# Opening loads in smaller parts, one of them on a second queue, and later weight splits queued differently in two attention mixers

## The chip, the cores and the metric

The kernel runs on one core of a Trainium2 chip. The metric is the device time of one execution, in microseconds (us). Before the change it is 977.02 us, the median of three runs (976.95 to 977.04).

## What is computed

A two-layer decoder trunk on 256 tokens of width 1024, all in float32. Layer 0 is a gated feed-forward half step, an attention mixer A (16 heads, a mixture of three dilated windows, which the kernel folds into one additive mask) and a second feed-forward half step. Layer 1 is the same with mixer B, whose keys and values come from one shared projection of layer 0's output. A last RMS norm follows.

```
def swiglu(h, w_gate, w_up, w_down):
    return (jax.nn.silu(h @ w_gate) * (h @ w_up)) @ w_down
...
for layer in range(DEPTH):
    h = h + 0.5 * swiglu(rmsnorm(h, ffn1_norm[layer]), ffn1_w_gate[layer], ffn1_w_up[layer], ffn1_w_down[layer])
    hn = rmsnorm(h, mix_norm[layer])
    h = h + mixer(hn)        # A or B: softmax attention, then @ w_o
    h = h + 0.5 * swiglu(rmsnorm(h, ffn2_norm[layer]), ffn2_w_gate[layer], ffn2_w_up[layer], ffn2_w_down[layer])
    if layer == 0:
        shared = shared_kv(h, kv_norm, kv_w, pos)
return rmsnorm(h, final_norm)
```

The hidden width of a feed-forward step is 2816, so its gate and up weights are 1024 x 2816 each.

## The kernel before

**Numbers in two parts.** Every product keeps float32 accuracy by splitting each operand into a coarse part and the rest. ScalarE makes the coarse part with a copy (`wh` of weights, `hi` of activations), VectorE subtracts it from the source (`wl`, `lo`), and TensorE adds up three products: coarse by coarse, coarse by rest, rest by coarse. So every weight passes through ScalarE and VectorE before TensorE may use it. `unit` (lines 152 to 169) loads 1 MB of weights with one DMA on SyncE's queue and splits it in two halves of 128 x 1024; `parts_of` (91 to 99) does the same for activations, and can put off VectorE's half.

**The stream of tokens.** `hT` holds the stream transposed, as eight blocks of 128 channels by 256 tokens. `Norm.scale` (236) multiplies a block by its gain and splits it into x; `Norm.square` (239) adds up the squares on the side; the norm's factor per token comes late and is applied to the products.

**The opening.** The first feed-forward step starts with nothing in memory. Its first two output columns of gate and up (f = 0 and 1) are therefore computed block by block, as the blocks of channels arrive: `ffn_blocks` (line 422 on) takes from `opening` (171 to 185), for each block k, the 128 x 256 parts of gate and up, and does four products of 512 columns (the coarse weights with both parts of x, line 204) and four of 256 columns (the rest of the weights, line 210) into four accumulators. The list OPENING (line 39) says how the blocks are put together: each pair (k, n) is a start and a number of blocks that share their DMAs, one buffer and one split. `first` (838 to 842) loads the x of those blocks on SyncE's queue and calls `scale` for each. The first block's weights are loaded ahead of everything on ScalarE's own DMA queue (110 to 112); they get a buffer named early. Buffers for raw weights come from a pool of four. While the first loads run, TensorE does nine matmuls on constants (117). After the blocks come the squares (line 433, ScalarE) and their additions (line 246, VectorE here), the first ordinary units for f = 2, and in the middle of its products the column sums of the norm (251).

A DMA on SyncE's queue signals one of eight semaphores in turn, and an issue waits until the DMA that last used its semaphore has landed.

**The mixers.** `mixer` (748) runs the projections and then `out_t` (613), the products of the attention's output o with w_o. The steps of the attention are put among these products by an agenda: `plan` lists for every group of four heads, at which time after its q and k are turned, which of the steps scores (s), turns (t) and values (v) of a pair of heads p is traced. `turn` (701) turns the weights of the attention, p, and splits them (706 and 709); `values` (713) computes po, which ScalarE (727) and VectorE (732) join to o; `close` splits o into the block oT (98 and 95), which `out_t` reads. The last three blocks are held back and taken together for each output.

**Order.** The order in which each engine gets its instructions is chosen when the program is built, by a scheduler that works with estimated costs; within an engine it is fixed. What the author adds to it is `queued` (144): instructions traced in its block come behind those kept under a name in `marks`, on the same engine, in order of issue only. `marks[p]` holds both halves of the split of p, `marks[("o", p)]` only VectorE's half of the split of o. The feed-forward step after a mixer names, for each half of its first units, what it is to stand behind: `queue` (lines 864 and 887) has the two halves of the first gate unit, the two of the first up unit, then those of the next units. LAST_O (line 38) is the last block o, pair 7.

Of the kernel before, what the change touches and what calls it, by code (L numbers as in the profile page):

```python
# [10 lines left out]
F32 = mybir.dt.float32  # L11
F32R = mybir.dt.float32r
AF = mybir.ActivationFunctionType
ALU = mybir.AluOpType

P = 128
S = 256
# [18 lines left out]
         ("ffn1_norm", 1), ("mix_norm", 1), ("ffn2_norm", 1)]  # L36

LAST_O = ("o", H // 2 - 1)
OPENING = ((0, 1), (1, 1), (2, 2), (4, 2), (6, 2))
GX = len(GAINS) * KD  # L40


# [25 lines left out]
def trunk(ctx: ExitStack, tc: tile.TileContext, a: dict, out: bass.AP):  # L68
    nc = tc.nc
    PS = bass.MemoryType.PSUM  # L70
    const = ctx.enter_context(tc.tile_pool(name="const", bufs=1))
    rawp = ctx.enter_context(tc.tile_pool(name="rawp", bufs=4))
# [18 lines left out]
    def parts_of(hi, lo, src, scale=1.0, later=None):  # L91

        def rest():
            if isinstance(scale, float):
                return nc.vector.tensor_sub(lo, src, hi.bitcast(F32))
            return nc.vector.scalar_tensor_tensor(lo, src, scale, hi.bitcast(F32), op0=ALU.mult, op1=ALU.subtract)  # L96

        nc.scalar.activation(hi, src, AF.Copy, scale=scale)  # L98
        (later or (lambda call: call()))(rest)

    def etile(name, dt=F32):
# [5 lines left out]

    both = const.tile([P, GX + KD * S], F32, name="gains_hT")
    gT, hT = both[:, :GX], both[:, GX:].rearrange("p (k s) -> p k s", s=S)
    early = rawp.tile([P, 2, OPENING[0][1], S], F32, tag="raw", name="raw_0_0")  # L110
    for i, n in enumerate(("gate", "up")):
        nc.scalar.dma_start(early[:, i], a[f"ffn1_w_{n}"][0][:OPENING[0][1] * P, :S].rearrange("(k p) n -> p k n", p=P))
    BF16 = mybir.dt.bfloat16
    fill = nc.const_aps.tensor(1.0, [P, 512], BF16)
    busy = trt("busy")
# [26 lines left out]
    marks = {}  # L142
# [28 lines left out]
    def opening(wg, wu, before):  # L171


        for k, n in OPENING:
            raw = rawp.tile([P, 2, n, S], F32, tag="raw", name=f"raw_0_{k}") if k else early
            wh, wl = [wp.tile([P, 2, n, S], F32R, tag=tag, name=f"{tag}_0_{k}") for tag in ("wh", "wl")]
            before(k, n)
            for i, w in enumerate((wg, wu)):
                if k:
                    nc.sync.dma_start(raw[:, i], rows(w, k, n, 0, S))  # L180
            for part in ([slice(0, 2)] if k else [slice(0, 1), slice(1, 2)]):
                marks["opening"] = [nc.scalar.activation(wh[:, part], raw[:, part], AF.Copy)]
            nc.vector.tensor_sub(wl, raw, wh.bitcast(F32))
            for j in range(n):
                yield [(wh[:, i, j, :], wl[:, i, j, :]) for i in range(2)]
# [276 lines left out]
    def ffn(name, layer, which, norm, after, first=None, beside=(), homes=("kx4", "kx6", "qkh", "qkh"), queue=()):  # L462
        wg, wu, wd = (a[f"ffn{which}_w_{n}"][layer] for n in ("gate", "up", "down"))
        sums = left_sums(homes)
        blocks = ffn_blocks(name, wg, wu, norm, first, beside, sums, queue)
        if which == 1:
            table(AF.Exp, blocks[-1][:, 0, 0:1].bitcast(F32))
        down(f"{name}_d", wd, blocks, sums, after)
# [193 lines left out]
    def attention(agenda, operands, mask, name, blocks):  # L662

        segs = [slice(t * P, t * P + (t + 1) * P) for t in range(NT)]
        owns = [slice(i * DH, (i + 1) * DH) for i in range(2)]
        sms, pTs = {}, {}

        def scores(p):
            g, b = divmod(p, HG // 2)
            (hi, lo), _ = operands(g)
            ps = [trt(f"s_{name}{p}_{i}") for i in range(2)]
            for t, seg in enumerate(segs):
                for n, (q, k) in enumerate(((hi, hi), (hi, lo), (lo, hi))):
                    for i, own in enumerate(owns):
                        nc.tensor.matmul(ps[i][:, seg], q[own, b, t, :],
                                         k[own, 2 + b].rearrange("p t n -> p (t n)")[:, :(t + 1) * P],
                                         start=n == 0, stop=n == 2)  # L680
            nm = sp.tile([P, 2, NT], F32, tag="nm", name=f"nm_{name}{p}")
            ls = sp.tile([P, 2, NT], F32, tag="ls", name=f"ls_{name}{p}")
            for i in range(2):
                sm = sms[p, i] = atile([P, 3 * P], name=f"sm_{name}{p}_{i}")
                for t, seg in enumerate(segs):
                    nc.vector.tensor_tensor_reduce(sm[:, seg], ps[i][:, seg], mask[:, seg], scale=-SCALE, scalar=3e38,
                                                   op0=ALU.add, op1=ALU.min, accum_out=nm[:, i, t:t + 1])
                agenda.after(0.7 + 0.7 * i, soften, sm, nm[:, i], ls[:, i])

        def soften(sm, nm, ls):  # L690
            for t, seg in enumerate(segs):
                nc.scalar.activation(sm[:, seg], sm[:, seg], AF.Exp, bias=nm[:, t:t + 1], scale=-1.0,
                                     accum_out=ls[:, t:t + 1])
            agenda.after(1.3, scale, sm, ls)

        def scale(sm, ls):
            nc.vector.reciprocal(ls, ls)  # L697
            for t, seg in enumerate(segs):
                nc.gpsimd.tensor_scalar(sm[:, seg], sm[:, seg], ls[:, t:t + 1], None, op0=ALU.mult)  # L699

        def turn(p, i):
            tr = trt(f"pt_{name}{p}_{i}")[:, :3 * P]
            for n in range(3):
                nc.tensor.transpose(tr[:, n * P:(n + 1) * P], sms[p, i][:, n * P:(n + 1) * P], ident)
            pT = pTs[p, i] = pp.tile([P, 2, 3 * P], F32R, tag="pT", name=f"pT_{name}{p}_{i}")
            hi = nc.scalar.activation(pT[:, 0], tr, AF.Copy)

            def rest():
                marks[p] = [hi, nc.vector.tensor_sub(pT[:, 1], tr, pT[:, 0].bitcast(F32))]

            agenda.soon(rest)

        def values(p):
            g, b = divmod(p, HG // 2)
            po = acc(f"po_{name}{p}")
            s = etile(f"o_{name}{p}")
            vs = operands(g)[1]
            acs = [po[:, i * S:(i + 1) * S] for i in range(2)]
            for i, ac in enumerate(acs):
                pT = pTs[p, i]  # L720
                v0, v1 = [flat(v[:, 2 * b + i]) for v in vs]
                for n in range(2):
                    nc.tensor.matmul(ac, v0, pT[:, n, :S], start=n == 0, stop=False)
                for n in range(2):
                    nc.tensor.matmul(ac[:, P:], v1, pT[:, n, S:], start=False, stop=n == 1)
            for own, ac in zip(owns, acs):
                nc.scalar.activation(s[own], ac[DH:], AF.Copy)
            agenda.soon(lambda: close(p, s, acs))

        def close(p, s, acs):  # L730
            for own, ac in zip(owns, acs):
                nc.vector.tensor_add(s[own], ac[:DH], s[own])
            x = atile([P, 2, S], F32R, name=f"oT_{name}{p}")

            def split():
                parts_of(x[:, 0], x[:, 1], s, later=lambda low: agenda.soon(lambda: marks.update({("o", p): [low()]})))

            agenda.soon(split)
            agenda.after(1.5, arrived, x)

        def arrived(x):
            blocks.append(x)
            if len(blocks) == KD:
                table(AF.Silu, x[:, 0, 0:1].bitcast(F32))

        return scores, turn, values
# [89 lines left out]


    def first(k, n):
        cols = slice(GX + k * S if k else 0, GX + (k + n) * S)
        nc.sync.dma_start(both[:, cols], a["gains_xT"][:, cols])  # L840
        for i in range(k, k + n):
            n0.scale(i)

    n0, n1, n2 = Norm(0, "n0", nc.vector), Norm(1, "n1"), Norm(2, "n2")
    n3, n5, n6 = Norm(4, "n3"), Norm(5, "n5"), Norm(6, "n6")
# [4 lines left out]
    w, n = a["a_w_qkv"][0], HG * DH  # L850
# [3 lines left out]
    def steps(g, *at):  # L854
        return [(wait, step, 2 * g + i) for wait, step, i in zip(at, "sstvtv", (0, 1, 0, 0, 1, 1))]

    def ending(at, apart=2.6):
        return [(at + apart * i + wait, step, 4 + i) for i in range(4) for wait, step in ((0.0, "t"), (2.3, "v"))]

    mixer("a", [qk[0], v[0], qk[1], qk[2], qk[3], v[1]],  # L860
          [steps(0, 3.0, 8.0, 11.0, 13.8, 16.5, 19.3), steps(1, 3.0, 8.0, 11.0, 13.8, 16.5, 19.3), steps(2, 4.0, 9.2),
           steps(3, 2.4, 5.4) + ending(8.4)],
          a["a_w_o"][0], masks[:, 0, :], n2, {3: 4, 4: 5})
    ffn("f20", 0, 2, n2, n3, queue=(5, 6, 7, 7) + (LAST_O,) * 4)
    kx = []
    ffn("f11", 1, 1, n3, n5, homes=("qkh", "qkh", "pT"), beside=[lambda k=k: kx.append(gain(k, 3, "kx", "kx")) for k in range(KD)])
    xkv, xq = by_token(kx), n5.xs()
# [88 lines left out]
```

## Time and profile before

| | us |
|---|---|
| median of three runs | 977.02 |
| the profiled execution | 979.19 |
| its span, first to last instruction | 977.4 |
| TensorE (PE) busy | 967.4 |
| weight loads of TensorE (PEld) busy | 833.1 |
| VectorE (DVE) busy | 813.2 |
| ScalarE (ACT) busy | 611.9 |
| GpSimd (POOL) busy | 281.4 |

The mean granted clock of TensorE over the span is 0.996 of full speed, and 174 MB are read from memory at a mean of 179 GB/s. Busy times overlap; only work that nothing else hides adds to the span. A line number such as L182 is a line of the kernel before. In the order of time, a row has its start, its length, the engine, the line, the operation, the tile written and those read, the shape, the count and in brackets how long the engine stood idle before it and what ended that; matmuls start before the one ahead of them has ended, so the distance between starts counts, not the length. Rows of a load have the issue; their last number in the list of DMAs is the time from issue to landing.

### The profile page before, as it was taken

How to read it: one execution, taken by the hardware profiler on the slowest of the kernel's cores; microseconds unless marked ns; L12 is line 12 of the kernel's file. 1: busy time of each engine (PE TensorE's matmuls, PEld its weight loads, DVE VectorE, ACT ScalarE, POOL GpSimd, SP SyncE). 2: the span in 40 equal slices, each digit the busy share in tenths (PEclk: the TensorE clock that was granted, in tenths of full speed). 3: DMA queues.
4: the chain of work that ended last, by engine and by line, in shares of the span. 5: the costliest groups of instructions: out<-in, count | busy, mean ns of one | idle time of the engine just before them, and what ended most of it. 6: DMA issues, size and time to landing. Idle time of an engine off the chain costs nothing.

```text
span 977.4 us, 14864 instructions
## 1 busy us (share of the span) xinstructions
PE 967.4 (99%) x5392; PEld 833.1 (85%) x5392; DVE 813.2 (83%) x1393; ACT 611.9 (63%) x1132; POOL 281.4 (29%) x235
## 2 busy tenths in 40 slices
PE   8999999999999999999999999999999999999997
PEld 6888888878889888888888888888888998888886
DVE  6988889887878788889898888987787778888996
ACT  7655657566777665556576655655577766666561
POOL 0211237133432211146032111622143322112451
PEclk9999999999999999999999999999999999999999
DMA  9875546664334666545855556483734345565341
GB/s 313 256 241 180 191 152 216 216 216 152 122 111 141 190 191 185 185 154 210 258 165 180 173 175 212 164 277 119 254 122 141 107 154 172 184 203 174 130 172 43
DMA packets 127145, 176.00 MB, mean 180 GB/s; under 512 B 3424, under 2 KB 106848, under 8 KB 127072
## 3 DMA queue, kind: packets, MB, share of 16 engines
q1 hardware_dynamic: 126496, 174.27, 54.9%
q8 instruction: 42, 0.69, 0.3%
q10 hardware_dynamic: 576, 0.79, 0.2%
q14 instruction: 31, 0.25, 0.1%
HBM read 173.99 MB, written 1.05 MB: 179 GB/s over the span
## 4 chain that ended last, share of the span: by engine, by line
PE 96%; DVE 1%; ACT 1%; DMA 1%; issue 0%; POOL 0%; POOLq 0%; DVEq 0%; ACTq 0%
PE f_g L204 17%; PE f_u L204 16%; PE f_u L210 9%; PE f_g L210 9%; PE dn_f_d L193 6%; PE dn_f_d L197 6%; PE dn_f_d L195 6%; PE dn_f_d_m L193 1%; PE dn_f_d_m L197 1%; PE dn_f_d_m L195 1%; PE qk_a L193 1%; PE qk_a L197 1%; PE qk_a L195 1%; PE v_a L193 1%; PE q_b L193 1%; PE ot_bo L624 1%
## 5 line engine op out<-in xcount | busy, mean ns | idle before, releaser
L386 POOL TENSOR_TENSOR j_f_u<-j_f_u,r_n 128x256 f32<-128x256 f32 x88 | 91.6, 1043 | 360.0 <-DVE j_f_u L342 339.5
L204 PE MATMUL f_g<-x_n,wh_f_g 128*128 128x512 f32 x688 | 180.6, 394 | 0.0
L204 PE MATMUL f_u<-x_n,wh_f_u 128*128 128x512 f32 x688 | 177.3, 390 | 0.0
L204 PEld LDWEIGHTS f_u<-x_n,wh_f_u 128*128 128x128 f32 x688 | 129.1, 188 | 27.2
L204 PEld LDWEIGHTS f_g<-x_n,wh_f_g 128*128 128x128 f32 x688 | 124.0, 189 | 22.8 <-DVE x_n L96 0.2
L166 DVE TENSOR_TENSOR wl_f_u<-raw_f_u,wh_f_u 128x1024 fp32r<-128x1024 f32 x86 | 113.5, 1323 | 0.8 <-ACT wh_f_u L165 0.8
L166 DVE TENSOR_TENSOR wl_f_g<-raw_f_g,wh_f_g 128x1024 fp32r<-128x1024 f32 x86 | 104.5, 1232 | 0.9 <-ACT wh_f_g L165 0.9
L210 PE MATMUL f_u<-x_n,wl_f_u 128*128 128x256 f32 x688 | 103.5, 283 | 0.0
L210 PE MATMUL f_g<-x_n,wl_f_g 128*128 128x256 f32 x688 | 102.9, 282 | 0.0
L210 PEld LDWEIGHTS f_g<-x_n,wl_f_g 128*128 128x128 f32 x688 | 96.4, 190 | 6.3
L165 ACT ACTIVATE wh_f_u<-raw_f_u 128x1024 fp32r<-128x1024 f32 x86 | 87.7, 1047 | 10.8 <-PE f_g L204 7.5
L384 ACT ACTIVATE j_f_g<-j_f_g 128x256 f32<-128x256 f32 x88 | 36.6, 417 | 89.1 <-DVE j_f_g L383 88.8
L165 ACT ACTIVATE wh_f_g<-raw_f_g 128x1024 fp32r<-128x1024 f32 x86 | 89.4, 1048 | 4.1 <-PE f_g L204 2.9
L210 PEld LDWEIGHTS f_u<-x_n,wl_f_u 128*128 128x128 f32 x688 | 91.8, 192 | 0.0
L246 POOL TENSOR_TENSOR ss_n<-ss_n,sq_n 128x256 f32<-128x256 f32 x35 | 32.5, 928 | 138.7 <-ACT sq_n L245 136.9
L98 ACT ACTIVATE act_f<-j_f_g 128x256 fp32r<-128x256 f32 x58 | 23.9, 418 | 56.5 <-DVE j_f_g L394 56.4
L394 DVE TENSOR_TENSOR j_f_g<-j_f_g,j_f_u 128x256 f32<-128x256 f32 x58 | 27.9, 486 | 29.9 <-POOL j_f_u L386 29.9
L342 DVE TENSOR_TENSOR j_f_g<-f_g,j_f_g 128x256 f32<-128x256 f32 x88 | 36.6, 416 | 11.9 <-ACT j_f_g L341 11.9
L699 POOL TENSOR_SCALAR sm_a<-sm_a,ls_a 128x128 f32<-128x128 f32 (+1 forms) x32 | 30.3, 964 | 47.8 <-DVE ls_a L697 42.1
L699 POOL TENSOR_SCALAR sm_b<-sm_b,ls_b 128x128 f32<-128x128 f32 (+1 forms) x32 | 29.1, 929 | 50.0 <-DVE ls_b L697 46.0
L341 ACT ACTIVATE j_f_u<-f_u 128x256 f32<-128x256 f32 x88 | 33.0, 375 | 14.6 <-PE row_n L263 13.6
L383 DVE TENSOR_TENSOR j_f_g<-j_f_g,r_n 128x256 f32<-128x256 f32 x88 | 41.4, 474 | 0.7
(565 smaller groups left out, 2387.3 us busy)
## 6 DMA issues: line engine op xcount, KB each, us to landing
raw_f_d<-in_ffn_w_down_dram SPq DMA_DIRECT2D x44, 1024.0 KB, 4.9
raw_f_g<-in_ffn_w_gate_dram SPq DMA_DIRECT2D x43, 1024.0 KB, 5.4
raw_f_u<-in_ffn_w_up_dram SPq DMA_DIRECT2D x43, 1024.0 KB, 5.4
raw_qka<-in_a_w_qkv_dram SPq DMA_DIRECT2D x16, 512.0 KB, 4.6
raw_va<-in_a_w_qkv_dram SPq DMA_DIRECT2D x4, 1024.0 KB, 6.1
raw_ao<-in_a_w_o_dram SPq DMA_DIRECT2D x4, 1024.0 KB, 4.9
raw_kvb<-in_kv_w_dram SPq DMA_DIRECT2D x8, 512.0 KB, 4.1
raw_qb<-in_b_w_q_dram SPq DMA_DIRECT2D x4, 1024.0 KB, 5.5
```

Source lines behind the costliest of these rows:

```text
L165: nc.scalar.activation(wh, r, AF.Copy)
L166: nc.vector.tensor_sub(wl, r, wh.bitcast(F32))
L193: nc.tensor.matmul(ac, xh, wh, start=first, stop=False)
L195: nc.tensor.matmul(ac, xh, wl, start=False, stop=False)
L197: nc.tensor.matmul(ac, xl, wh, start=False, stop=last)
L204: nc.tensor.matmul(ac, wh, flat(x), start=first and i == 0, stop=False)
L210: nc.tensor.matmul(ac[:, :S], wl, x[:, 0, :], start=False, stop=last and i == len(ws) - 1)
L342: nc.vector.tensor_add(s, ac[:, :S], s)
L383: nc.vector.tensor_mul(g, g, norm.row)
L384: nc.scalar.activation(g, g, AF.Silu)
L386: nc.gpsimd.tensor_tensor(u, u, norm.row, op=ALU.mult)
L699: nc.gpsimd.tensor_scalar(sm[:, seg], sm[:, seg], ls[:, t:t + 1], None, op0=ALU.mult)
```

## The change

Three parts.

*Opening.* Blocks 2 and 3 are no longer one entry of OPENING but two, each with its own weight DMAs, its own part of a buffer and its own split (128 x 512 instead of 128 x 1024). The first four blocks share one raw buffer, singles. The x of blocks 2 and 3 is loaded with one DMA as before, but on ScalarE's queue behind the first block's weights, and `first` leaves it out. In the built program, SyncE's queue has for these blocks gate 2, up 2, gate 3, up 3 where it had x, gate and up of both; ScalarE's queue has three DMAs ahead of its first work where it had two; the loads of the first ordinary unit and of its up half wait for other buffers. On TensorE, block 2's matmuls of coarse weights and rest alternate.

*Marks.* The function that `parts_of` hands to `later` returns both instructions, and the mark of an o keeps both: splits queued behind the last o stand behind ScalarE's copy too.

*Queue and plan.* After mixer A the second half of the first gate unit stands behind p 7, where it stood behind p 6. The values of pair 1 in mixer A are planned at 19.8 where they were at 19.3.

In the built program this gives, on ScalarE in mixer A: copy of o (pair 6), then the copies of the first gate unit's second half and of the up unit's two, then the joining of the last o and its copy, then the next unit's copy, then the loading of a function table. Before, the gate unit's second half stood right behind the last but one p, and the next unit's copy behind the table. VectorE's rests follow the same order. In mixer B, the next unit's first copy moves from ahead of the joining of the last o to behind the copy of it. The products po of pair 1 in mixer A come three matmuls of the projection later. GpSimd's order is unchanged.

```
-OPENING = ((0, 1), (1, 1), (2, 2), (4, 2), (6, 2))
+OPENING = ((0, 1), (1, 1), (2, 1), (3, 1), (4, 2), (6, 2))
...
         def rest():
             if isinstance(scale, float):
-                return nc.vector.tensor_sub(lo, src, hi.bitcast(F32))
-            return nc.vector.scalar_tensor_tensor(lo, src, scale, hi.bitcast(F32), op0=ALU.mult, op1=ALU.subtract)
+                return first, nc.vector.tensor_sub(lo, src, hi.bitcast(F32))
+            return first, nc.vector.scalar_tensor_tensor(lo, src, scale, hi.bitcast(F32), op0=ALU.mult, op1=ALU.subtract)
 
-        nc.scalar.activation(hi, src, AF.Copy, scale=scale)
+        first = nc.scalar.activation(hi, src, AF.Copy, scale=scale)
         (later or (lambda call: call()))(rest)
...
-    early = rawp.tile([P, 2, OPENING[0][1], S], F32, tag="raw", name="raw_0_0")
+
+    def load_x(engine, k, end):
+        cols = slice(GX + k * S if k else 0, GX + end * S)
+        engine.dma_start(both[:, cols], a["gains_xT"][:, cols])
+
+    singles = rawp.tile([P, 4, 2, S], F32, tag="raw", name="raw_0")
     for i, n in enumerate(("gate", "up")):
-        nc.scalar.dma_start(early[:, i], a[f"ffn1_w_{n}"][0][:OPENING[0][1] * P, :S].rearrange("(k p) n -> p k n", p=P))
+        nc.scalar.dma_start(singles[:, 0, i], a[f"ffn1_w_{n}"][0][:P, :S])
+    load_x(nc.scalar, 2, 4)
...
         for k, n in OPENING:
-            raw = rawp.tile([P, 2, n, S], F32, tag="raw", name=f"raw_0_{k}") if k else early
+            raw = rawp.tile([P, 2, n, S], F32, tag="raw", name=f"raw_0_{k}") if n > 1 else singles[:, k:k + 1].rearrange("p k i n -> p i k n")
...
             def split():
-                parts_of(x[:, 0], x[:, 1], s, later=lambda low: agenda.soon(lambda: marks.update({("o", p): [low()]})))
+                parts_of(x[:, 0], x[:, 1], s, later=lambda low: agenda.soon(lambda: marks.update({("o", p): low()})))
...
     def first(k, n):
-        cols = slice(GX + k * S if k else 0, GX + (k + n) * S)
-        nc.sync.dma_start(both[:, cols], a["gains_xT"][:, cols])
+        if k not in (2, 3):
+            load_x(nc.sync, k, k + n)
         for i in range(k, k + n):
             n0.scale(i)
...
     mixer("a", [qk[0], v[0], qk[1], qk[2], qk[3], v[1]],
-          [steps(0, 3.0, 8.0, 11.0, 13.8, 16.5, 19.3), steps(1, 3.0, 8.0, 11.0, 13.8, 16.5, 19.3), steps(2, 4.0, 9.2),
+          [steps(0, 3.0, 8.0, 11.0, 13.8, 16.5, 19.8), steps(1, 3.0, 8.0, 11.0, 13.8, 16.5, 19.3), steps(2, 4.0, 9.2),
...
-    ffn("f20", 0, 2, n2, n3, queue=(5, 6, 7, 7) + (LAST_O,) * 4)
+    ffn("f20", 0, 2, n2, n3, queue=(5, 7, 7, 7) + (LAST_O,) * 4)
```

## The prediction, on record before the changed kernel was run

> **What bounds the kernel now.** I read the page's first part, then the chain of waits at the opening, then busy time and granted clock by stage.
>
> ```profile
> span 977.4 us, 14864 instructions
> PE 967.4 (99%) x5392; PEld 833.1 (85%) x5392; DVE 813.2 (83%) x1393; ACT 611.9 (63%) x1132; POOL 281.4 (29%) x235
> ```
>
> TensorE is busy in 99% of the span, so a gain must come from its few waits. The profiled execution took 979.19 us, 1.79 more than its span and 2.17 more than the median of 977.02; I take the differences found in the span off the median.
>
> ```profile
> 0.72 3.02 DMA raw<-in_ffn_w_gate_dram
> 3.75 5.43 DMA raw<-in_ffn_w_up_dram
> 9.20 1.06 ACT wh L182
> ...
> 11.14 0.43 PE f_g L204
> ...
> 20.56 1.83 PE f_g L204 x8
> ...
> 22.73 0.70 PE f_g L210 x5
> ...
> 30.70 0.95 PE f_g L210 x8
> ```
>
> The chain (start, us, what) starts with loads: the up half of blocks 2 and 3 is issued at 3.75, lands at 9.18, is split by ScalarE, and only then TensorE goes on without a break. At 20.56 the opening's eight blocks are done. A matmul of 512 columns takes 1.83/8 = 0.23 us there, one of 256 columns 0.95/8 = 0.12; a block has four of each, 1.40 us. But at 11.14 a matmul of 512 took 0.43.
>
> ```profile
> 4.19:7.60 3.41, 2.93 (x14) 1.93 (x13) 2.56 (x6) 2.53 (x6) 0.00 (x0) 1.00 0.92 310
> 7.60:11.02 3.42, 1.59 (x9) 1.09 (x8) 1.15 (x3) 1.82 (x3) 0.00 (x0) 0.96 1.04 351
> 11.02:14.43 3.41, 3.41 (x14) 2.88 (x13) 3.25 (x6) 2.73 (x5) 0.00 (x0) 0.54 1.10 357
> ```
>
> Columns: stretch, length, busy PE, PEld, DVE, ACT, POOL, granted clock, DMA share, GB/s. PE is busy for 2.93 of 3.41 us (86%) before 7.60, then for 1.59 of 3.42 (46%), and in the stretch after that the clock is about half. So the late block costs twice: its gap, and some 1.7 us of half speed.
>
> **The opening, part by part.** Blocks 2 and 3 come one by one; their x goes on ScalarE's queue.
>
> ```profile
> GB/s 0 0 86 309 357 202 290 369 335 317 296 344 367 381 380 370 354 347 348 350 350 347 350 347 350 345 350 347 351 347 345 336 371 343 348 176 143 366 382 380
> 3.05 0.43 SPq L180 DMA_DIRECT2D raw<-in_ffn_w_gate_dram  x1
> raw<-in_ffn_w_gate_dram SPq DMA_DIRECT2D x1, 256.0 KB, 4.2
> ...
> 3.56 0.51 ACT L98 ACTIVATE x_n<-gains_hT 128x256 fp32r<-128x256 f32 x1 [0.42 <-DMA gains_hT<-in_gains_xT_dram]
> ```
>
> Rates are in steps of 0.75 us: about 350 GB/s but for a dip to 202 and 290 between 3.75 and 5.25. Bytes and their order decide. Block 2's last part now stands 1.31 MB into the order (x 156+128, the first two blocks' weights 512, x of 2 and 3 256, block 2's 256 KB) instead of 1.56. The gate half of blocks 2 and 3 stood there before and landed at 3.05 + 4.2 = 7.25. From the other side, 256 KB at 350 GB/s off 9.18 gives 8.45. I take 7.3, the row with the same bytes ahead; block 3 follows between 8.2 and 9.2. Cost: SP issues one DMA more (four weight parts for two, one x fewer) at 0.43 us, well ahead of need. ScalarE issues one more before its first work; it idles 0.42 there until block 0's x lands, and that covers it; uncovered it would be 0.43 on every block's start. The first unit's gate half no longer waits for a buffer and its up half waits only for block 3's rest; both stand behind the blocks in the queue, so this is worth nothing here. GpSimd's queue is untouched.
>
> The Trainium skill's page "Trainium Kernel Development and Optimization" (Key Constraints) speaks against the second queue: all queues run on the same 16 DMA engines, so a second issuer only saves issue time. By that rule the last landing would not move and the opening would give 0.2 us less; the trace half agrees, with a DMA share of 0.92 in the stretch to 7.60.
>
> ```profile
> 5.87 0.63 ACT L182 ACTIVATE wh<-raw 128x512 fp32r<-128x512 f32 x1 [0.69 <-DMA raw<-in_ffn_w_up_dram]
> 6.53 0.69 DVE L183 TENSOR_TENSOR wl<-raw,wh 128x512 fp32r<-128x512 f32 x1 [0.63 <-ACT wh L182]
> 10.31 0.49 PE L204 MATMUL f_g<-x_n,wh 128*128 128x512 f32 x1 [1.83 <-ACT wh L182]
> 11.38 1.06 ACT L182 ACTIVATE wh<-raw 128x1024 fp32r<-128x1024 f32 x1 [0.32 <-DMA raw<-in_ffn_w_up_dram]
> 13.59 1.06 ACT L182 ACTIVATE wh<-raw 128x1024 fp32r<-128x1024 f32 x1 [0.36 <-DMA raw<-in_ffn_w_up_dram]
> 14.68 1.23 DVE L183 TENSOR_TENSOR wl<-raw,wh 128x1024 fp32r<-128x1024 f32 x1 [0.20 <-ACT wh L182]
> 15.82 3.07 DVE L246 TENSOR_TENSOR ss_n<-ss_n,sq_n 128x256 f32<-128x256 f32 x6
> 20.28 1.22 DVE L166 TENSOR_TENSOR wl_f_g<-raw_f_g,wh_f_g 128x1024 fp32r<-128x1024 f32 x1
> ```
>
> Walk forward. Block 2: split 0.63 from 7.35, rest 0.69, ready at 8.7; block 1 ends near 8.5 (10.31 less the 1.83 of waiting). PE loses 0.2 there and block 2 runs to 10.0. Block 3, landing at 8.7, is ready at 10.0 and runs to 11.4 (11.7 if it lands at 9.2). The 1.83 us gap goes, and PE is busy from 7.60 to 11.02. Late next: blocks 4 and 5, landing at 11.3 as before (same bytes ahead): split to 12.4, rest to 13.6. Block 4 waits 1.0 us, and after three matmuls 0.5 more, to run with block 5 to 15.7. Blocks 6 and 7 bound the end: I take their landing as 13.4 instead of 13.5, since a third of the dip is filled; + 1.06 + 1.23 = 15.7, after which 1.17 of block 6 and 1.40 of block 7 remain: 18.3 instead of 20.56. VectorE then sets the pace: its additions start at 15.6 (0.2 earlier), and the six, the next unit's rest, the seventh and the second rest end at 21.3 instead of 21.5. PE needs that for the fifth L210, in the chain at 22.73 + 4 x 0.14 = 23.3; from the opening's end to that point are 2.17 + 0.56 us of its own work, so it gets there at 21.0 and waits to 21.3. **Gain 2.0 us**, 0.3 below what the opening's end alone gives.
>
> ```profile
> 22.77 0.16 DVE L253 TENSOR_SCALAR v_n<-col_n 128x2 f32<-128x2 f32 x1 [1.27 <-PE col_n L251]
> 35.65 1.22 DVE L166 TENSOR_TENSOR wl_f_u<-raw_f_u,wh_f_u 128x1024 fp32r<-128x1024 f32 x1
> 37.22 0.96 PE f_u L210 x8
> ```
>
> Does it last? VectorE's wait of 1.27 goes too, so it comes 1.5 us earlier. The tightest rest later ended at 36.87, needed by the fifth of eight at 37.7; now 35.4 against 35.7. It holds by 0.3; beyond, PE alone sets the pace.
>
> **The mixers.** Returning both instructions adds none. The marks of the last o now hold ScalarE's copy too, and the second half of mixer A's first unit waits behind the last p. The first half stays behind p 5, so its stall of p 6 stays. In the changed order the second half's copy and rest stand among the two of the up unit, ahead of the last o.
>
> ```profile
> 294.63 2.00 ACT L165 ACTIVATE wh_f_u<-raw_f_u 128x1024 fp32r<-128x1024 f32 x2
> 295.72 2.36 DVE L166 TENSOR_TENSOR wl_f_u<-raw_f_u,wh_f_u 128x1024 fp32r<-128x1024 f32 x2 [0.21 <-ACT wh_f_u L165]
> 298.00 0.84 DVE L732 TENSOR_TENSOR o_a<-po_a,o_a 64x256 f32<-64x256 f32 x2
> 298.87 0.42 ACT L98 ACTIVATE oT_a<-o_a 128x256 fp32r<-128x256 f32 x1 [1.18 <-DVE o_a L732]
> 299.32 0.42 DVE L95 TENSOR_TENSOR oT_a<-o_a,oT_a 128x256 fp32r<-128x256 f32 x1 [0.48 <-ACT oT_a L98]
> 300.37 0.28 PE L624 MATMUL ot_ao<-oT_a,wh_ao 128*128 128x256 f32 x1
> ```
>
> VectorE has three rests instead of two from 295.72, at 1.14 each (2.36 less 1.22): o_a starts at 299.14 instead of 298.00, the copy ends at 300.4, its rest at 300.9. PE needs the copy at 300.37 and the rest 0.12 later: **0.4 us lost**. Bounds: 0, if PE comes there later; 1.14, if none of the slack were there. What the move frees, ScalarE and VectorE around 290 to 293, held nobody. The v of p 1 moves behind three more matmuls, 0.7 us:
>
> ```profile
> 235.50 0.78 ACT L727 ACTIVATE o_a<-po_a 64x256 f32<-64x256 f32 x2 [1.67 <-PE po_a L725]
> ```
>
> Between 0 and 0.7 us; ScalarE idles 1.67 ahead of it, and its o is read only by the o products that follow all projections. I take nothing.
>
> ```profile
> 778.50 1.06 ACT L165 ACTIVATE wh_f_g<-raw_f_g 128x1024 fp32r<-128x1024 f32 x1 [0.52 <-PE ot_bo L625]
> 779.58 0.77 ACT L727 ACTIVATE o_b<-po_b 64x256 f32<-64x256 f32 x2
> 779.13 0.34 PE L725 MATMUL po_b<-pT_b,vs_b 128*128 128x128 f32 x2
> 781.74 0.38 PE L624 MATMUL ot_bo<-oT_b,wh_bo 128*128 128x256 f32 x1 [0.19 <-ACT oT_b L98]
> ```
>
> In mixer B a copy of 1.06 leaves the place ahead of o_b. The last po ended at 779.47, 0.1 before o_b, so o_b comes 0.1 us earlier, and with it the last oT_b, for which PE waited at 781.74: **0.1 gained** (at least nothing, at most the 0.2 of that wait). The copies pushed behind the last o delay the first x of the next stage by up to 1.1 us, hidden by the 60 o products of 0.12 us still to run, 7 us.
>
> **Sum:** -2.0 + 0.4 - 0.1 = -1.7, so 975.3.
>
> **Rivals.** The last up half of the opening took 6.8 us from issue to landing:
>
> ```profile
> raw<-in_ffn_w_up_dram SPq DMA_DIRECT2D x1, 256.0 KB, 6.8
> ```
>
> 1. *The clock falls one stretch later.* From 11.02 to 14.43 PE would now be busy for 0.4 + 0.7 + 0.8 us and some 0.5 of tails, 56% to 70%; 46% lost the clock, 86% kept it. If it falls, the stretch to 17.84 runs at half: 1.7 us back, **977.0**. The Trainium skill's page "TensorE: Matmul & The Clock Gate" (What's actually happening) has the clock halve after at least one idle window of some 3.4 us. By that rule this rival had no chance; the trace disagrees, since the clock fell after a wait of 1.83.
> 2. *The mixers cost nothing or gain*, since PE comes to the last o later than I think: **974.9**.
> 3. *Too few bytes in flight* (slower). An issue on SP waits until the DMA eight back has landed. With halves, eight hold less. If all parts took 6.8 us like that one, the last would be issued when block 2's up half lands (3.75 + 6.8 = 10.55) and land at 17.4; PE would end the opening at 22.3, 1.7 late: **979.0**. It decides from a last landing after 15.4. Against it: early parts took 4.2.
> 4. *Block 2's landing does not move* from 9.2, gap and clock stay: **977.3**, the mixers' loss alone. Against it: 256 KB less are ahead.
>
> **How the numbers follow.** Forecast 0.50 (974.8 to 975.9 by itself), rival 1 0.18, rival 2 0.22, rival 3 0.04, rival 4 0.06. The range leaves out the far part of rival 2 below and rivals 3 and 4 above: 974.5 to 977.1. A difference under 0.2% (1.95 us) is about what a measurement cannot tell from none. Faster by more needs 975.07: most of rival 2 and a quarter of the forecast, 0.34. Slower by more than 978.97: rival 3 and mishaps, 0.05. Same 0.61.
>
> **What would show it.** Right: no PE gap near 8.5 to 10.3, granted clock 1.00 from 11.02 to 17.8, end of the opening near 18.3, and in mixer A a PE wait of 0.4 for the last oT_a. Wrong: a clock of 0.5 from 14.43; a landing of blocks 6 and 7 far from 13.4; a rest of the next units that PE awaits between 20 and 40 us; no wait, or over 0.6, at the last o.

## The result, and the profile after

| | us, median | lowest to highest | executions |
|---|---|---|---|
| before, same series | 977.03 | 976.80 to 977.66 | 22 |
| after | 978.67 | 977.67 to 980.38 | 22 |

The ratio is 1.0016, 95% interval 1.0010 to 1.0023: slower by 1.6 us, where 1.7 less were forecast. The time lies 1.6 above the upper end of the range.

The page of after, first part (TensorE's busy time is again 99% of the span):

```profile
span 976.7 us, 14869 instructions
PE 966.9 (99%) x5392; PEld 831.9 (85%) x5392; DVE 812.7 (83%) x1394; ACT 611.2 (63%) x1133; POOL 282.0 (29%) x235
```

This span is 0.7 shorter than the one of before that the prediction read (977.4), and the profiled execution took 978.46, close to its median. So one profile against the other says faster, and the medians say slower. The execution of before with the profile took 979.19 against a median of 977.03; it is the odd one.

Busy time by stretch in after (PE, PEld, DVE, ACT, POOL, granted clock, DMA share, GB/s):

```profile
7.60:11.02 3.42, 3.42 (x20) 2.78 (x19) 3.00 (x7) 2.13 (x5) 0.00 (x0) 1.00 0.85 241
11.02:14.43 3.41, 2.47 (x13) 1.63 (x12) 1.92 (x3) 2.18 (x4) 0.00 (x0) 1.00 1.01 310
14.43:17.84 3.41, 3.34 (x19) 2.65 (x19) 2.51 (x5) 3.40 (x10) 0.00 (x0) 1.00 1.09 365
```

The gap between 8.5 and 10.3 is gone and the clock stays at 1.00, as predicted; block 2's copy starts at 7.39 (7.35 was worked out). But the DMA engines moved 241 GB/s from 7.60 to 11.02, where before they moved 351, and TensorE waits in the next stretch instead. The chain of waits tells why:

```profile
1.64 4.52 DMA gains_hT<-in_gains_xT_dram
6.18 0.38 SPq L186
...
8.10 5.99 DMA raw<-in_ffn_w_up_dram
14.11 1.07 ACT wh L188
15.20 1.24 DVE wl L189
...
19.34 1.86 PE f_g L210 x8
```

The x of blocks 2 and 3, on ScalarE's queue since 1.64, lands at 6.16. Only then does SyncE issue the gate half of blocks 4 and 5, at 6.18. In the profile of before it went out at 4.68:

```profile
4.68 0.43 SPq L180 DMA_DIRECT2D raw<-in_ffn_w_gate_dram  x1
```

Its semaphore is the one of that x. By the times of the releases, the eight semaphores are taken in turn over both queues, not over SyncE's alone: the issue at 3.75 in before came when block 0's gate half landed, which is on ScalarE's queue (0.72 + 3.02). All issues behind it are late too. Block 1 is later as well: ScalarE's copy of it starts at 6.45 instead of 5.87, and TensorE is busy for 2.15 us from 4.19 to 7.60 instead of 2.93. The last up half lands at 14.1 (13.4 was predicted, 13.45 in the profile of before), and the opening ends at 19.34 (18.3 predicted).

The last o of mixer A in after, VectorE's rows and then TensorE's:

```profile
294.74 1.23 DVE L172 TENSOR_TENSOR wl_f_g<-raw_f_g,wh_f_g 128x1024 fp32r<-128x1024 f32 x1 [0.21 <-ACT wh_f_g L171]
295.88 2.35 DVE L172 TENSOR_TENSOR wl_f_u<-raw_f_u,wh_f_u 128x1024 fp32r<-128x1024 f32 x2
298.15 0.84 DVE L738 TENSOR_TENSOR o_a<-po_a,o_a 64x256 f32<-64x256 f32 x2
299.47 0.43 DVE L95 TENSOR_TENSOR oT_a<-o_a,oT_a 128x256 fp32r<-128x256 f32 x1 [0.48 <-ACT oT_a L98]
```

```profile
299.26 0.28 PE L632 MATMUL ot_ao<-oT_a,wl_ao 128*128 128x256 f32 x1
299.49 0.39 PE L630 MATMUL ot_ao<-oT_a,wh_ao 128*128 128x256 f32 x1
299.95 0.39 PE L631 MATMUL ot_ao<-oT_a,wh_ao 128*128 128x256 f32 x1
```

Three rests now stand ahead of o_a, and TensorE's steps, 0.12 elsewhere in these products, are 0.23 and 0.46 here: 0.45 of waiting, for the copy and then for the rest of the last oT. In mixer B the wait of 0.19 for oT_b is gone (no bracket now):

```profile
781.12 0.38 PE L630 MATMUL ot_bo<-oT_b,wh_bo 128*128 128x256 f32 x1
```

### The profile page after: what moved, and what is told of

Read it like the earlier page. It is cut to its first block, busy times and chain, and to the rows that moved or that the text cites. A ratio compares the mean times of both kernels' runs of the same rounds, so it can differ in the third digit from the quotient of the medians.

```text
span 976.7 us, 14869 instructions
## 1 busy us (share of the span) xinstructions
PE 966.9 (99%) x5392; PEld 831.9 (85%) x5392; DVE 812.7 (83%) x1394; ACT 611.2 (63%) x1133; POOL 282.0 (29%) x235
## 4 chain that ended last, share of the span: by engine, by line
PE 95%; DVE 2%; DMA 1%; ACT 1%; issue 1%; SPq 0%; POOL 0%; ACTq 0%; POOLq 0%; DVEq 0%
PE f_g L210 16%; PE f_u L210 16%; PE f_g L216 8%; PE f_u L216 8%; PE dn_f_d L203 6%; PE dn_f_d L199 6%; PE dn_f_d L201 6%; PE dn_f_d_m L203 1%; PE dn_f_d_m L199 1%; PE dn_f_d_m L201 1%; PE qk_a L199 1%; PE qk_a L203 1%; PE qk_a L201 1%; PE v_a L199 1%; PE q_b L199 1%; PE ot_bo L630 1%
```

## The experiments

Three series on one chip each; before was run in all of them (977.21, 977.15 and 977.23). The 95% intervals of single ratios are about 0.09% (0.9 us) to each side, so for parts of half a microsecond the traces carry the argument and the medians support it: the intervals of e1, e2 and e4 all include no change. "Matmul against matmul" below means the distance in time between the starts of the same matmul in two traces.

### The kernel before, profiled again (b0_before)

No edit was made.

> The kernel before, unchanged, to see more of its executions. Theory A (the execution whose profile was read had lost the clock in the opening, and the timed executions do not): its profile here shows a granted clock of 1.00 in the stretch from 11.02 to 14.43, the opening's eight blocks done near 18.8 instead of 20.56, a span near 975.3, and the time stays 977.0. Theory B (the timed executions lose the clock too, and the change loses its time somewhere else): the clock is again near 0.54 there, the opening ends at 20.5, the span is 977.4 and the time near 979.

Measured: 977.45 (eleven executions; nine from 976.86 to 977.54, two at 978.96 and 979.13), span 975.7. Stretches, and rows of the chain:

```profile
7.60:11.02 3.42, 2.04 (x10) 1.16 (x8) 1.61 (x3) 2.03 (x4) 0.00 (x0) 1.00 1.02 357
11.02:14.43 3.41, 3.36 (x20) 2.99 (x21) 3.10 (x6) 3.08 (x6) 0.00 (x0) 1.00 1.10 358
```

```profile
8.70 1.06 ACT wh L182
9.79 1.23 DVE wl L183
...
18.80 1.85 PE f_g L204 x8
```

Theory A holds. Blocks 2 and 3 landed at 8.7 here, 0.5 earlier than in the first profile; TensorE was busy for 60% of the stretch, kept its clock, and ended the opening at 18.80 instead of 20.56. From there on the two executions run with the same distance, 1.75 us: the later landing and the half clock together. Matmul against matmul of this trace, after is 0.75 late at 60 us, 1.3 behind mixer A, and 1.15 at the end.

### Block 2 still later (e5_late_block2, e8_later_block2)

```
# first(k, n), e5: at k == 2 load the x of blocks 2 to 5, none at 4
-        cols = slice(GX + k * S if k else 0, GX + (k + n) * S)
-        nc.sync.dma_start(both[:, cols], a["gains_xT"][:, cols])
+        if k != 4:
+            cols = slice(GX + k * S if k else 0, GX + (k + n + (2 if k == 2 else 0)) * S)
+            nc.sync.dma_start(both[:, cols], a["gains_xT"][:, cols])
# e8: at k == 2 load the x of blocks 2 to 7, none at 4 and 6
```

> The kernel before, with the x of blocks 4 and 5 loaded together with that of blocks 2 and 3, so 256 KB more stand ahead of block 2's weights and none more ahead of block 4's. Block 2 should land 0.7 later than 8.68, near 9.4, and TensorE be busy for some 1.4 of 3.42 us (41%) in the stretch from 7.60 to 11.02. If a stretch under about half busy costs the clock in the next one (46% lost it, 60% and 67% kept it), the granted clock is 0.5 from 11.02 to 14.43, the opening ends near 20.7 and the time is 979.0 or more. If the clock of 0.54 in the first profile had another cause, the clock stays 1.00, the opening ends near 19.1 and the time is under 977.6.

> The kernel before with the x of blocks 4 to 7 loaded with that of blocks 2 and 3, so 512 KB more than before stand ahead of block 2's weights; nothing more ahead of the last blocks'. With 256 KB more the executions fell into two groups, 977.7 to 978.1 (six) and 979.6 to 980.6 (five), and the profiled one, in the first group, had kept its clock. If the second group are executions that lost the clock in the stretch from 11.02 to 14.43 because TensorE idled too long before it, nearly all executions are now in it, at 979.5 to 981, and the profile shows a granted clock near 0.5 in that stretch. If the groups have another cause, the profile keeps 1.00 there, and the time is under 978.5.

Measured: e5 978.14, but in two groups, six executions from 977.71 to 978.14 and five from 979.57 to 980.55. The profiled one is of the first group. e8: 980.46 (978.43 to 982.26). First e5's stretch, then e8's:

```profile
7.60:11.02 3.42, 2.09 (x10) 1.40 (x10) 2.69 (x5) 3.04 (x6) 0.00 (x0) 1.00 1.08 367
```

```profile
7.60:11.02 3.42, 1.46 (x8) 1.01 (x8) 2.35 (x5) 3.36 (x7) 0.00 (x0) 1.00 1.10 363
11.02:14.43 3.41, 3.41 (x13) 2.62 (x12) 3.41 (x5) 3.23 (x7) 0.00 (x0) 0.55 1.10 347
```

In e8 TensorE was busy for 43% of the stretch, and the next ran at 0.55: the trace ends 1.88 later than that of b0. The mean clock of every execution is on record too, and one stretch of 3.41 us at half lowers a mean over 977 us by 0.0017. In e5 the first group has 0.998 or 0.999 and the second 0.996 or 0.997. In e8 five of eight have 0.995 or 0.996; the other three kept 0.998 or 0.999 and still took 978.43, 979.01 and 980.96. So "nearly all" was not met, and e8 lost time in another way as well, which was not followed up. e5's expectation of all executions at 979.0 or more failed: it sits on the edge, the copy of block 2 starting at 8.94 in the profiled execution, not at 9.4. That copy did not wait for its weights: ScalarE first had the x of four blocks to scale, from 7.32 on.

So the kernel before has the same two kinds of execution, with the longer one rare: 6 of 126 executions in all series took over 978.9, and these six have a mean clock of 0.996 or 0.997 where the others of their series have 0.998 or more. The first profile, with 0.996, had caught one.

### The opening alone (e1_opening), on SyncE's queue (e3_opening_sp), and the second queue alone (e9_x_act)

```
# e1: the change's opening; returns of parts_of, marks, plan and queue of before
# e3: e1, but
-    load_x(nc.scalar, 2, 4)
...
-        if k not in (2, 3):
-            load_x(nc.sync, k, k + n)
+        if k != 3:
+            load_x(nc.sync, k, 4 if k == 2 else k + n)
# e9: before, but
+    nc.scalar.dma_start(both[:, GX + 2 * S:GX + 4 * S], a["gains_xT"][:, GX + 2 * S:GX + 4 * S])
...
+        if k != 2:
+            nc.sync.dma_start(both[:, cols], a["gains_xT"][:, cols])
```

> The opening's part of the change alone (blocks 2 and 3 in weight parts of their own, their x on ScalarE's queue); marks, queue and plan of the mixers as before. Theory A: slower than before, 977.5 to 978.3, since its opening ends at 19.3 against 18.8. Theory B: faster by about 1, 976.0, as the opening's end moved from 20.56 to 19.34 between the two profiles.

> The opening's part alone, but with the x of blocks 2 and 3 on SP's queue ahead of block 2's weights. If the second queue is what delays block 1's up half (5.82 before, 6.45 after), block 1 lands at 5.8 again and the time is 0.5 under that of the opening alone. If the count of DMAs in flight is what delays the last blocks (the issue that waits for the DMA eight back, a dip to 174 GB/s near 8 to 10), the last up half still lands near 14.1 and the time is that of the opening alone within 0.3.

> The kernel before with only the x of blocks 2 and 3 moved to ScalarE's queue; weights in the parts of before. If the second queue alone costs the 0.7 between the two split openings (978.03 with it, 977.34 with SP's), the time is 977.7 or more. If it costs only where halves make more DMAs stand between an issue and the DMA eight back that it waits for, the last landing stays within 0.2 of 13.04 and the time within 0.3 of before.

Measured: e1 978.03 (before 977.21), e3 977.34 (977.21), e9 977.14 (977.23). What SyncE waited for until 9 us, in e1 and then in e3:

```profile
SPq L186 <- DMA gains_hT<-in_gains_xT_dram: 1.1, 1, 1.1
...
SPq L186 <- DMA raw<-in_ffn_w_gate_dram: 0.6, 1, 0.6
```

```profile
SPq L185 <- DMA raw<-in_ffn_w_gate_dram: 0.4, 2, 0.3
```

What the DMA engines moved from 7.5 to 10.6 us in b0, after, e1 and e3, in this order:

```profile
DMA packets 944, 1.10 MB, mean 355 GB/s; under 512 B 67, under 2 KB 748, under 8 KB 944
```

```profile
DMA packets 649, 0.72 MB, mean 233 GB/s; under 512 B 46, under 2 KB 547, under 8 KB 649
```

```profile
DMA packets 719, 0.83 MB, mean 267 GB/s; under 512 B 51, under 2 KB 578, under 8 KB 719
```

```profile
DMA packets 816, 0.95 MB, mean 306 GB/s; under 512 B 60, under 2 KB 645, under 8 KB 816
```

The wait alone does not lower the rate. In e9 SyncE waited for 1.4 us (0.9 for that x, 0.5 for a gate half), and the DMA engines moved 371 GB/s in the same stretch. There the gate and up halves of blocks 4 and 5 had gone out at 4.43 and 4.98, ahead of the long wait; in e1 they stood behind it, at 6.52 and 6.94. With the x on SyncE's queue 0.4 of waiting is left in place of 1.7, block 1's up half lands at 6.1 instead of 6.8, and the last one near 13.2 instead of 13.9. With the second queue but the old pairs, the last half landed at 12.5 and nothing is lost. The Trainium skill's page "Trainium Kernel Development and Optimization" (Key Constraints) has a second queue save issue time alone; e9 agrees (977.14 against 977.23). So neither edit costs by itself. With halves more DMAs stand ahead of blocks 4 and 5, and so their gate half is the issue that has to wait for the x of blocks 2 and 3; on ScalarE's queue that x goes beside everything else and lands only at 6.2 (after) or 6.5 (e1). That the rate falls because fewer bytes are then under way fits these traces, but no run tests it apart. e3 was expected 0.5 under e1 with block 1 landing at 5.8; it came 0.7 under, with 6.1. e9's expectation for the second theory (last landing within 0.2 of 13.04) was missed on the good side; that landing varies between executions.

Why e3 does not gain, though its opening ends half a microsecond before b0's. Its copy of the last weights and two of VectorE's rows, then its chain:

```profile
13.25 1.06 ACT L187 ACTIVATE wh<-raw 128x1024 fp32r<-128x1024 f32 x1 [0.40 <-DMA raw<-in_ffn_w_up_dram]
```

```profile
15.49 3.07 DVE L251 TENSOR_TENSOR ss_n<-ss_n,sq_n 128x256 f32<-128x256 f32 x6
...
19.94 1.22 DVE L171 TENSOR_TENSOR wl_f_g<-raw_f_g,wh_f_g 128x1024 fp32r<-128x1024 f32 x1
```

```profile
18.31 1.84 PE f_g L209 x8
20.15 0.53 PE col_n L256 x4
```

In b0 the second rest and the matmuls that need it are these:

```profile
19.73 1.22 DVE L166 TENSOR_TENSOR wl_f_g<-raw_f_g,wh_f_g 128x1024 fp32r<-128x1024 f32 x1
```

```profile
20.85 0.85 PE L210 MATMUL f_g<-x_n,wl_f_g 128*128 128x256 f32 x5
```

The last landing sets VectorE's additions and the next unit's second rest, which ends at 21.16 (in b0 20.95). TensorE's column sums take 0.53 instead of 0.34, the next five matmuls are stretched as well, and of 0.5 at 18 us 0.1 remains at 22 us, matmul against matmul. Where the last half landed earlier, at 12.6 (e2) and 12.5 (e9), the trace keeps its whole lead over b0 past 60 us, 0.42 and 0.45.

### The mixers alone (e2_mixers), and the marks alone (e4_marks)

```
# e2: returns of parts_of, marks, 19.8 and queue (5, 7, 7, 7) of the change, opening of before
# e4: e2 with plan (19.3) and queue of before
-    ffn("f20", 0, 2, n2, n3, queue=(5, 7, 7, 7) + (LAST_O,) * 4)
+    ffn("f20", 0, 2, n2, n3, queue=(5, 6, 7, 7) + (LAST_O,) * 4)
```

> The mixers' part alone (both instructions in the marks, queue 5, 7, 7, 7, and 19.8 for 19.3); opening as before. Both traces set side by side give 0.5 lost at the last o of mixer A and 0.2 gained at the end of mixer B. Theory A: 977.2 to 977.5. Theory B, under which the loss that the two openings do not explain lies here: 978.7 to 979.3.

> Only the marks of the change (the mark of an o holds the copy and the rest); queue 5, 6, 7, 7, the plan and the opening as before. If the queue is what costs at the last o of mixer A (one rest more of 1.14 ahead of it), the 0.5 lost there in both traces with queue 5, 7, 7, 7 is gone, the 0.1 to 0.2 gained in mixer B stays, and the time is 0.1 to 0.2 under before. If the marks cost it, 0.5 is lost at the last o again, and the time is 0.3 over before.

Measured: e2 977.71 (before 977.21), e4 977.30 (977.15). Matmul by matmul, e2 falls back 0.55 against b0 around the last o of mixer A and wins 0.09 at the end of mixer B. e2's median lies 0.2 above theory A's range and far below theory B's. In e4 only two rests stand at that place:

```profile
293.96 2.36 DVE L166 TENSOR_TENSOR wl_f_u<-raw_f_u,wh_f_u 128x1024 fp32r<-128x1024 f32 x2 [0.21 <-ACT wh_f_u L165]
```

and nothing is lost there; at the end of mixer B it wins 0.07. Its median is 0.15 over before, where 0.1 to 0.2 under was expected; such a step is too little for the medians, but it is in every trace with the marks (0.07 to 0.09 in after, e2, e4, e6, e10 and e11) and in none without them. The queue entry that was 6 and became 7 is what costs, not the marks. The queue was not run without the plan's 19.8; at the pair that 19.8 moves, near 235 us, e2 and b0 differ by less than 0.1.

### Where VectorE binds, and a better version (e7_adds_pool, e6_both, e10_early_squares, e11_split_each)

```
# e7: e3 with Norm(0, "n0", nc.vector) -> Norm(0, "n0"): additions on GpSimd
# e6: e3 with the change's returns of parts_of and marks
# e10: e6, with the squares of blocks 0 to 3 ahead of the products of blocks 2 and 3
+                    if first is not None and 2 <= k < 4:
+                        norm.square(2 * k - 4)
+                        norm.square(2 * k - 3)
...
-                        for k in range(KD):
+                        for k in range(4, KD):
# e11: e4 (pairs of before), with e10's squares, and in opening
+            for j in range(n):
+                for part in ([slice(0, 2)] if k else [slice(0, 1), slice(1, 2)]):
+                    marks["opening"] = [nc.scalar.activation(wh[:, part, j], raw[:, part, j], AF.Copy)]
+                nc.vector.tensor_sub(wl[:, :, j], raw[:, :, j], wh[:, :, j].bitcast(F32))
+                yield [(wh[:, i, j, :], wl[:, i, j, :]) for i in range(2)]
```

> The split opening with x on SP's queue, and the seven additions of the first norm on GpSimd in place of VectorE. In the split opening alone the gain over before shrinks from 0.5 at 18 us to 0.2 at 20 us, after the opening's end. If VectorE's additions ahead of the next unit's rest are what takes it back, the 0.5 stays or grows with the additions away, and the time is 0.3 or more under that of the split opening alone. If GpSimd's additions (0.93 each, 6.5 in all) are late for the first norm's column, or slow VectorE, TensorE waits near 20 to 27 us and the time is above before.

> Candidate: the split opening with the x of blocks 2 and 3 on SP's queue, and the marks, with queue and plan as before. If the parts add up: 0.4 off the span of before in the opening and 0.1 to 0.2 in mixer B, so 0.2 to 0.5 under before. If the opening's part is given back by VectorE before 25 us, only the 0.1 to 0.2 of mixer B remain.

> The candidate with split opening, x on SP's queue and the marks, and with the first norm's squares and additions of blocks 0 to 3 done before the last weights land, not behind the opening's last copy. In the split opening TensorE had 0.5 at 18 us, and 0.35 of it went again while it waited for VectorE (additions, then the two rests of the next unit, done at 21.08). If VectorE's additions after the last landing are what takes it, three of them (0.51 each) are gone from there, the second rest ends near 19.9 and the 0.5 stays: 0.3 under the candidate without it, 976.9 to 977.0. If the additions do not bind, 977.3 as without it.

> The loads of before (pairs, x on SP's queue), but each block split into copy and rest by itself (0.63 and 0.69 in place of 1.06 and 1.23 from a landing to the first matmul with the rest), early squares, and the marks. Block 2 lands at 8.7 as before; TensorE goes on at 9.4 instead of 9.81 and stays busy, ending the opening near 17.9 instead of 18.80; the second rest of the next unit ends near 19.9 and is not waited for. If so, 0.9 is gained and the time is 976.3. If bytes or VectorE bound the end after all, under 0.3 is gained: 976.9 or more.

Measured: e7 979.78, e6 977.34 (both beside 977.15), e10 976.86, e11 976.29 (both beside 977.23; ratio of e11 0.9991, interval 0.9983 to 1.0000). In e7 the additions on GpSimd came too late: TensorE stood still for 2.24 us, until 22.84, for the last of them, where it had not before:

```profile
17.84:21.25 3.41, 2.76 (x12) 1.64 (x10) 2.81 (x2) 3.41 (x6) 3.20 (x3) 1.00 1.10 349
21.25:24.67 3.42, 1.83 (x14) 1.79 (x15) 1.33 (x5) 2.81 (x4) 2.17 (x3) 1.00 1.10 348
```

So e7 cannot show what VectorE without additions is worth, and e10 moves some of the additions ahead instead. VectorE's rows in e10:

```profile
16.01 2.00 DVE L251 TENSOR_TENSOR ss_n<-ss_n,sq_n 128x256 f32<-128x256 f32 x4
17.93 2.35 DVE L171 TENSOR_TENSOR wl_f_g<-raw_f_g,wh_f_g 128x1024 fp32r<-128x1024 f32 x2
```

Its last half landed late, at 13.78, yet the second rest ends at 20.28: 6.5 behind the landing, against 7.9 in e3. The time is 0.48 under that of e6, run in another series (0.3 was expected), which the intervals do not tell from nothing; the earlier rest is what the trace shows. e6's gain of at most 0.5 did not show. e11 gains 0.94 in the median, as worked out (0.9). But its profiled execution is again an odd one, 979.29 with block 2 landing at 9.86, so no trace shows whether its opening otherwise ends near 17.9, as the working has it:

```profile
7.60:11.02 3.42, 1.31 (x8) 0.91 (x7) 1.74 (x5) 1.74 (x5) 0.00 (x0) 1.00 1.04 370
11.02:14.43 3.41, 3.41 (x14) 2.92 (x13) 3.41 (x8) 3.16 (x8) 0.00 (x0) 0.54 1.10 352
```

e11 is the fastest version run, one execution in eleven aside; e10 kept to 976.55 to 977.50. Both together were not run.

## Why the prediction was wrong

1. **The base of the sum: this is the step that failed.** "I take the differences found in the span off the median." The profiled execution was 2.17 over the median, and the prediction gave that number without asking what it was. It was the very stall that the change removes: a landing 0.5 late and a stretch at half the clock, 1.75 us together against b0. The timed executions did not have it, so its removal could not be taken off their median. The change may well remove the rare stall (none of the 22 executions of after has a mean clock under 0.998), but six in 126 do not move a median. Where the sum had -2.0 for the opening, the trace of after gives -1.0 against the first profile and +0.75 against b0's.
2. **The opening's landings.** The gap at 8.5 went, and the clock stayed, as said. The landing of the last half was put at 13.4, on a count of bytes; it came at 14.1. One issue more on SyncE was counted at 0.43 us, well ahead of need; in after the last up half is issued at 8.10 instead of 6.66. The row that spoke of it was in the prediction, as rival 3: an issue waits for the DMA eight back. The rival was worked out for one case far off (all parts at 6.8 us) and with a threshold of 15.4 that was measured against an end of 20.56. In b0 the last half landed at 13.0, and the second rest ended at 20.95 where TensorE came to it near 21.4; so, as an estimate from these rows, a last landing past some 13.5 already costs.
3. **VectorE sets the pace** at the next unit's rests: right, and the reason that e3 gains nothing.
4. **Mixer A**: 0.4 predicted; 0.45 in the two waits shown, 0.55 in all in after and in e2. Right, with the place.
5. **Mixer B**: 0.1 predicted, 0.08 in after, 0.09 in e2. Right.
6. **Rival 1** did not happen: 72% busy from 11.02 to 14.43, and the clock stayed. The forecast's 56 to 70% was not far off, but a stretch at 60% (b0) already keeps the clock (below).

With the base mended, the prediction's own terms would have given +0.3 for the mixers and nothing for the opening, whose second rest it put at 21.3, where b0's TensorE wants it near 21.4: 977.3, still 1.3 short. The late landing is 0.75 of that by the traces and 0.8 by e1, and the mixers cost 0.1 to 0.2 more than worked out. The parts measured alone, +0.8 (e1) and +0.5 (e2), make 1.3 of the 1.6, each within its interval of nothing; the traces of b0 and after make 1.15. These are two single executions: the one of b0 took 977.45, 0.42 over the median of before beside the result, and the one of after 978.46, 0.21 under its own. So the distance between these two, 1.0, is smaller than that of the medians, 1.6, by just what the two lie off.

## What to carry to other kernels

A profile is one execution: when its own time lies further from the median than the effect looked for, find in the trace what makes it odd before taking anything out of it, or the change is credited with mending what the timed executions do not have. A smaller first transfer is not free where issues wait for an older DMA in turn: count the DMAs between each issue and the one whose semaphore it needs, on all queues together. And a queue entry that lets a split run later moves its whole length in front of whatever comes next on that engine.

## What the hardware showed that was not expected

In the opening, the granted clock of a stretch of 3.41 us went with how busy TensorE was in the stretch before. From 7.60 to 11.02, 38% (e11), 43% (e8) and 46% (the first profile) cost the clock, 0.54 to 0.55 in the next stretch; 54% (e4), 60% (b0), 61% (e5) and 67% (e2) did not. But the clock's own stretches lie elsewhere in each execution. The traces have it at half from 10.78 to 14.19 in the first profile, from 11.33 to 14.74 in e8 and from 11.31 to 14.72 in e11. Counted on in such steps from the start of the full clock in its trace (5.29 and 5.60), e4 and e5 were never under 67% and 68% in the opening. And the share does not settle it alone: by the same count (from 5.37) e7 was busy for 1.58 of 3.41 us from 19.02 to 22.43 and kept the clock, which the first profile lost after 1.59. So no bound can be given.

The Trainium skill's page "TensorE: Matmul & The Clock Gate" (What's actually happening) has the clock halve after at least one idle window; if that means wholly idle, the runs disagree, since no stretch of the opening was. The late block and the lost clock together put the three traces 1.75 to 1.9 us behind that of b0.

The same loads in the same order did not land at the same time. The last part of block 2 in kernels with the loads of before landed at 8.2 (e2), 8.6 (e4), 8.7 (b0), 9.2 (the first profile) and 9.9 (e11); the two latest are the two that lost the clock. Whether that scatter alone decides it, or also where the clock's stretches happen to lie, is open.
